# A streaming encoder layer on one core: a tile made 32 bytes longer, three stores on another queue, four row loads twenty ticks later

## The chip, the cores and the metric

The kernel runs on one core of one Trainium2 chip. The metric is the device time of one execution in microseconds (us), taken as the median of several runs. One core has five engines that the profile names: PE (matmuls), DVE and POOL (elementwise work), ACT (activations, casts and copies) and SP (which here only issues DMAs). Each engine carries out its own list of instructions in order, and a semaphore wait of one instruction holds back all that stand behind it on the same engine. An engine that issues a DMA has it in that list too. SBUF is the on-chip memory of 128 partitions; a tile's place is told as a byte offset within each partition. PSUM holds the results of matmuls in banks.

## The reference

One layer for 1152 rows of tokens: 1024 of one new stream and 8 times 16 of running streams, with a width of 1024. All is float32.

```
h = x @ w_in                                # one input projection: all branch columns and two merge gates
z, xbc, dt, q, k, v, f, g_path, mg_m, mg_a = split(h)
y_m = rmsnorm(ssd_scan(silu(conv(xbc)), softplus(dt)) * silu(z))    # Mamba-2 branch, width 2048
o   = softmax(q k^T / 8 + c_t - c_s) v                              # attention with forget gates, 16 heads
y_a = o * silu(g_path)                                              # width 1024
u   = sigmoid(mg_m + b) * (y_m @ w_br_m) + sigmoid(mg_a + b) * (y_a @ w_br_a)
out = layer_norm(alpha * x + u @ w_out)     # and k, v, log f, conv and SSD states as further outputs
```

## The kernel before, in words

**Products.** A float32 product is made of three matmuls. Each operand is split in a high part (a cast to the type fp32r) and a low part (the rest), and high x high, high x low and low x high are summed in one PSUM bank. So each weight tile needs a cast on ACT and a subtraction on DVE or POOL, and so does each tile of rows. `passes`, `dense`, `quarter` and `whole` make such products for 384 token columns at a time (there are three such column groups, c = 0, 1, 2); there the weights are the stationary operand and the rows the moving one.

**Stages, in PE's order.** (1) The value projection (L333 to L335): 432 matmuls of 128 x 512. Here X, the input, is stationary, and the moving operand is the value weight: `vh` and `vl`, the two parts of `wv`, 512 columns of one of them at a time. (2) Eight groups of the SSD scan, with the projections that they need (`d`, `z`, convolutions) and small float32 matmuls (`tp`, `dS`, `y`, `up`). (3) Eight head pairs of attention (`s`, `st`, `o`; for the running streams `ss`, `so`), among them the merge gates: `gate_dense(j)` multiplies X with one tile of gate weights, and for each column group ACT takes tanh from PSUM into a tile `gate` (L851), and SP stores it to DRAM as `gate_d` (L852). Gate 14 is the last of them in the attention loop, gate 15 follows after the loop's pools are closed. (4) The merge of the SSD branch: the first quarter of its sixteen row tiles (kt 8 to 11, `A0`, matmuls `dq`); then `unit()`, which multiplies the middle eight row tiles' quadrants in seven products where eight would be plain, in four parts p = 0 to 3 (matmuls u0d, u0m and so on to u3m); then the last quarter (kt 12 to 15, `A1`, `dq` again). (5) The attention branch's merge (`yb1`, L245 to L247 again). (6) The output projection (`out`, L1612 to L1614, 128 x 512 with u stationary and the weights `woh`, `wol` moving) and the layer norm.

**Order.** Nearly all of it runs in `tc.manual_schedule()`, which takes instructions in the order in which the code writes them; on each engine the program keeps that order. `flow` runs generators beside the products: every second k step of a product is one tick, and a generator that yields n gets on again n ticks later, so that its instructions are written between those of the product. A part p of `unit()` has 22 ticks, the unit 88.

**Pieces of weights in the unit.** `prepare()` makes one piece of the weight quadrants, 32 in all. The T pieces are first a difference of two quadrants (L1425; on POOL for p = 0, on DVE later); then ACT casts the high part (L1427) and POOL subtracts the low part (L1428). The raw weights `wu` of the next part are loaded by SP (L1410) once the pieces T4 and T3 of this part are made. What comes out of PSUM is added to `acc` by DVE (L1449).

**Rows of the last quarter.** `rows_c01` handles the row tiles kt = 12 to 15 during the unit. `send` (L1361, L1364) has SP load the rows `yr` and, for even kt, a row `rsb` of norm factors spread to all partitions; `scaled` (L1368, DVE) multiplies by them; `parted` (L1509 on ACT, L1510 on DVE) splits two of the three column groups in high and low part. They are read first by the `dq` matmuls behind the unit. For the first quarter `load_rows` does the like (L1276, L1281, L1288, L1304).

**Where tiles lie.** The pool `s1` gives out offsets one after another. `ones`, 32 floats a partition, stands ahead of `cw`, `cb`, `cst`, `ceo`, of the value weights and raw loads of stage 1, and of the SSD stage's tiles. All of these end with the SSD stage. The first of the value weights, vh for k = 0, begins at byte 105,344 of its partition, which is a multiple of 64; each of these tiles begins at a multiple of 64. X, the weight tiles `wh` and `wl`, and every tile of the later stages begin 32 bytes past one: `woh` and `wol` are among them. `pre` is a small tile of the attention's set-up at the start of the SSD stage: an exclusive running sum over eight blocks (L500 clears its first block), read once.

Of the kernel before, what the change touches and what calls it, by code (L numbers as in the profile page):

```python
# [11 lines left out]
F32 = mybir.dt.float32  # L12
# [7 lines left out]
P = 128  # L20
# [14 lines left out]
GATES_SSD = 4  # L35
GATES_FOX = 4
# [113 lines left out]
def trunk_step(ctx: ExitStack, tc: tile.TileContext, I, O):  # L150
    nc = tc.nc
    ve, ac, po, te, sy = nc.vector, nc.scalar, nc.gpsimd, nc.tensor, nc.sync
# [20 lines left out]
    def ch(c):  # L173
        return slice(c * CW, (c + 1) * CW)
# [11 lines left out]
    gate_d = dr.tile([16, P, T], F32, name="gate_d")  # L186
# [73 lines left out]
    def dense(rhs, evac):  # L260

        hi, lo = next_w()
        for c in range(NCH):
            d = bank(f"d{count[0]}_{c}")[:, :CW]
            passes(d, KT, lambda k: (hi[:, k * P:(k + 1) * P], lo[:, k * P:(k + 1) * P]),
                   lambda k: (rhs[c][0][:, k, :], rhs[c][1][:, k, :]), lambda: evac(c, d))
# [5 lines left out]
    s1 = ssd_stack.enter_context(tc.tile_pool(name="s1", bufs=1))  # L272
# [3 lines left out]
    ea = s1.tile([P, 8, 32], F32, name="ea")  # L276
    eas = s1.tile([P, 8, 32], F32, name="eas")
    xac = s1.tile([P, 32], F32, name="xac")
    ones = s1.tile([P, 32], F32, name="ones")
    cw = s1.tile([P, 32, 4], F32, name="cw")  # L280
    cb = s1.tile([P, 32], F32, name="cb")
    ncol = I["const"].shape[1]
# [9 lines left out]
    pp = pro_stack.enter_context(tc.tile_pool(name="pp", bufs=1, side="right"))  # L292
# [4 lines left out]
    sfx = pp.tile([P, SEQ + 1], F32, name="sfx")  # L297
    nsf = pp.tile([P, SEQ], F32, name="nsf")
    catm = pp.tile([P, 9, 48], F32, name="catm")
    ff = pp.tile([16, P], F32, name="ff")  # L300
    pre = pp.tile([P, 8, 16], F32, name="pre")
    acf = pp.tile([32, T], F32, name="acf")
    cpro = pp.tile([P, I["const2"].shape[1]], F32, name="cpro")
    fones = pp.tile([P, P], F32, name="fones")
# [539 lines left out]
        if g == 7:  # L844
            square_rows(g, square_sums(g, "t"))

    def gate_dense(j, pool, tag, bufs):

        def evac(c, d):
            t = pool.tile([P, CW], F32, tag=tag, name=f"gate{j}_{c}", bufs=bufs)  # L850
            ac.activation(t[:], d, AF.Tanh, bias=bcol[:, j:j + 1])  # L851
            sy.dma_start(gate_d[j][:, ch(c)], t[:])  # L852

        dense(X, evac)

# [6 lines left out]
    def q_and_gate(hp):  # L862

        fp = lazy["f0"] if hp % 2 == 0 else lazy["fp"]
        r = {}
        qh = r["qh"] = fp.tile([P, SEQ], F32R, tag="qh", name=f"qh{hp}", bufs=1)
        ql = r["ql"] = fp.tile([P, SEQ], F32R, tag="ql", name=f"ql{hp}", bufs=1)
        qbd = r["qbd"] = fp.tile([P, 8, 2, 16], F32, tag="qbd", name=f"qbd{hp}", bufs=1)
        po.memset(qbd[:], 0.0)

        def evac_q(c, d):
            a, b = halves(c)
            ac.copy(qh[:, b], d[:, a])
            ve.tensor_tensor(ql[:, b], d[:, a], qh[:, b].bitcast(F32), ALU.subtract)
            if c == 2:
                for e in range(2):
                    hr = slice(64 * e, 64 * e + 64)
                    ac.copy(qbd[hr, :, e, :], d[hr, 256:].rearrange("p (b w) -> p b w", w=16))

        dense(X, evac_q)  # L880
        gs = r["gs"] = (fp if hp % 2 == 0 else lazy["fq"]).tile([P, T], F32, tag="gs", name=f"gs{hp}", bufs=1)
        silu_dense(fp, None, None, None, whole=gs)
        return r

    def keys(hp, r):
        fp = lazy["fp"]
        kh = r["kh"] = fp.tile([P, SEQ], F32R, tag="kh", name=f"kh{hp}", bufs=1)
        kl = r["kl"] = fp.tile([P, SEQ], F32R, tag="kl", name=f"kl{hp}", bufs=1)
        knew = r["knew"] = fp.tile([P, P], F32, tag="knew", name=f"knew{hp}", bufs=2)

        def evac_k(c, d):
            a, b = halves(c)
            kf = fp.tile([P, CW], F32, tag="kv1", name=f"kf{hp}_{c}", bufs=3)
            ac.copy(kf[:], d)
            sy.dma_start(O["k"][hp][:, ch(c)], kf[:])
            if c == 2:
                po.tensor_copy(knew[:], kf[:, 256:])
            ac.copy(kh[:, b], d[:, a])
            ve.tensor_tensor(kl[:, b], d[:, a], kh[:, b].bitcast(F32), ALU.subtract)

        dense(X, evac_k)
        return r
# [313 lines left out]
    for j in range(GATES_SSD):  # L1216
        gate_dense(j, spa, "z", 9)
# [30 lines left out]
    with tc.manual_schedule():  # L1248
        r = keys(0, r)
        for hp in range(1, 8):  # L1250
            flow.start(pair(hp - 1, r))
            gate_dense(GATES_SSD + hp - 1, fp, "kv1", 3)
            r = keys(hp, q_and_gate(hp))
        flow.start(pair(7, r))
        for j in range(GATES_SSD + 7, GATES_SSD + 7 + GATES_FOX):
            gate_dense(j, fp, "kv1", 3)
        flow.drain()
    fp_stack.close()

# [98 lines left out]
    def send(kt, rb, pool=mp, tag="rsb"):  # L1358

        y = mp.tile([P, T], F32, tag="yr", name=f"yr1{kt}", bufs=4)  # L1360
        sy.dma_start(y[:], ym_d[kt])  # L1361
        if kt % 2 == 0:
            rb[0] = pool.tile([P, T], F32, tag=tag, name=f"rsb{kt}", bufs=1)
            sy.dma_start(rb[0][:], rs_d[kt // 2:kt // 2 + 1, :].to_broadcast([P, T]))  # L1364
        return y

    def scaled(kt, y, rb):
        ve.scalar_tensor_tensor(y[:], y[:], mcol[:, kt:kt + 1], rb[0][:], ALU.mult, ALU.mult)  # L1368
# [138 lines left out]
    def parted(i, c):  # L1507
        h, l = A1[c][0][:, i, :], A1[c][1][:, i, :]
        ac.copy(h, ys[i][:, ch(c)])  # L1509
        ve.tensor_tensor(l, ys[i][:, ch(c)], h.bitcast(F32), ALU.subtract)  # L1510

    def rows_c01():

        rb = [None]
        for kt in range(12, 16):
            ys.append(send(kt, rb))
            yield 6
            scaled(kt, ys[-1], rb)
            yield 4
            parted(kt - 12, 0)  # L1520
            parted(kt - 12, 1)
            yield 4

    def rows_c2():

# [4 lines left out]
    with tc.manual_schedule():  # L1530
        prepare()
        for i in range(4):
            put("S4", i, s4[i][:])
        flow.start(rows_c01())
        todo.pop(0)
        unit()
        flow.drain()
# [54 lines left out]
    for c in range(NCH):  # L1592
# [27 lines left out]
        for j in range(3):  # L1620
            b, w = 3 * c + j, width[j]
# [108 lines left out]
```

## Time and profile before

| | us |
|---|---|
| median of 3 runs | 2019.84 (2019.16 to 2020.88) |
| profiled execution, whole time | 2018.57 |
| its span, first instruction to last | 2016.7 |
| PE busy | 2005.7 (99%) |
| DVE, ACT, POOL busy | 1301.0, 913.5, 530.7 |
| value projection on PE | from about 10 to 115 |
| SSD stage | to about 963 |
| attention | to about 1600 |
| gate 15 and first quarter | to about 1668 |
| unit | to about 1762 |
| last quarter, attention merge | to about 1880 |
| output projection and layer norm | to 2016.7 |

In the lists of instructions the first number is the start in us from the start of the span, the second the time from start to end, for a group "x3" over all three. Brackets give the idle time ahead of an instruction and what ended it. Matmuls overlap: one that is shown with 0.34 us is followed by the next after 0.17, so that PE's pace is read from start to start. SPq and ACTq are the issuing of DMAs on SP and ACT; "DMA" in the chain of waits is the transfer.

### The profile page before, as it was taken

Reading aid. Unit: us, or ns where it says so; the run is one execution under the profiler, and the core shown is the slowest. Engines: PE = TensorE matmul, PEld = TensorE weight load, DVE = VectorE, ACT = ScalarE, POOL = GpSimd, SP = SyncE. Lnnn points to the kernel's source line nnn. Section 1 sums busy time; section 2 is a strip of 40 time slices with the busy share of each in tenths; the row PEclk is TensorE's granted clock in tenths of the full one; section 3 lists DMA queues with packets and bytes.
Section 4 is the critical chain, followed back from the end, with each engine's and each line's share of the span. In section 5 each row is a group of like instructions: output and inputs, shape, how many; then the busy total and the mean of one; then the engine's idle time right before and its main releaser. Section 6 shows DMA issues by size and latency. Waiting matters only on the chain.

```text
span 2016.7 us, 36178 instructions
## 1 busy us (share of the span) xinstructions
PE 2005.7 (99%) x14247; PEld 1859.7 (92%) x14247; DVE 1301.0 (65%) x2165; ACT 913.5 (45%) x1971; POOL 530.7 (26%) x708
## 2 busy tenths in 40 slices
PE   9999999999999999999999999999999999999998
PEld 7899999999999999999988988988888999999987
DVE  5145766766667676643577787787786687582355
ACT  5125555554655656543545545455545353221210
POOL 0012445354535454523011001000100005414400
PEclk9999999999999999999999999999999999999999
DMA  7422242424233323343566566566656573164322
GB/s 225 157 75 90 67 145 68 133 80 131 82 127 90 126 87 123 96 135 107 182 214 199 191 218 195 170 213 203 191 190 203 189 273 114 57 232 137 98 92 94
DMA packets 123627, 292.51 MB, mean 145 GB/s; under 512 B 18633, under 2 KB 74945, under 8 KB 113217
## 3 DMA queue, kind: packets, MB, share of 16 engines
q1 hardware_dynamic: 110912, 208.93, 32.4%
q10 hardware_dynamic: 12544, 81.27, 11.6%
q8 instruction: 112, 1.84, 0.4%
q14 instruction: 59, 0.48, 0.1%
HBM read 233.64 MB, written 56.51 MB: 144 GB/s over the span
## 4 chain that ended last, share of the span: by engine, by line
PE 92%; DVE 3%; ACT 1%; DMA 1%; issue 1%; POOL 1%; SPq 0%; ACTq 0%; DVEq 0%; POOLq 0%
PE d L245 19%; PE d L247 18%; PE d L246 18%; PE s L951 3%; PE o L1026 3%; PE dq L245 2%; PE y L736 2%; PE dq L247 2%; PE dq L246 2%; PE out L1614 2%; PE out L1613 2%; PE out L1612 2%; PE v L334 2%; PE v L335 2%; PE v L333 2%; PE so L1101 2%
## 5 line engine op out<-in xcount | busy, mean ns | idle before, releaser
L245 PE MATMUL d<-xh,wh 128*128 128x384 f32 x2112 | 735.6, 348 | 0.0
L247 PE MATMUL d<-xh,wl 128*128 128x384 f32 x2112 | 707.3, 335 | 0.0
L246 PE MATMUL d<-xl,wh 128*128 128x384 f32 x2112 | 706.7, 335 | 0.0
L245 PEld LDWEIGHTS d<-xh,wh 128*128 128x128 f32 x2112 | 396.7, 188 | 19.7 <-issue 8.1
L246 PEld LDWEIGHTS d<-xl,wh 128*128 128x128 f32 x2112 | 397.3, 188 | 0.8
L247 PEld LDWEIGHTS d<-xh,wl 128*128 128x128 f32 x2112 | 396.5, 188 | 0.0
L225 POOL TENSOR_TENSOR wl<-wr,wh 128x1024 fp32r<-128x1024 f32 x45 | 107.7, 2394 | 200.0 <-ACT wh L224 199.2
L956 ACT ACTIVATE st<-s,ckt 128x256 f32<-128x256 f32 (+1 forms) x320 | 115.1, 467 | 19.4 <-PE s L951 17.0
L224 ACT CAST wh<-wr 128x1024 fp32r<-128x1024 f32 x56 | 58.7, 1049 | 119.9 <-PE d L246 94.4
L1016 ACT ACTIVATE st<-st 128x1024 f32<-128x1024 f32 x80 | 83.2, 1062 | 38.9 <-DVE st L1011 36.2
L960 POOL TENSOR_TENSOR st<-st,mask_bf 128x256 f32<-128x256 f32 x64 | 49.3, 791 | 195.4 <-ACT st L956 195.3
L705 ACT ACTIVATE m<-ce,nacum 128x128 f32<-128x128 f32 x288 | 96.9, 391 | 5.7 <-PE y L736 5.7
L228 DVE SCALAR_TENSOR_TENSOR wl<-wr,wh 128x1024 fp32r<-128x1024 f32 x50 | 62.7, 1255 | 33.3 <-ACT wh L227 33.3
L1428 POOL TENSOR_TENSOR pc<-wu,pc 128x512 fp32r<-128x512 f32 x32 | 43.2, 1360 | 127.3 <-ACT pc L1427 127.3
L632 POOL TENSOR_TENSOR wx<-xdt,wdt 128x256 f32<-128x256 f32 x72 | 54.0, 751 | 84.7 <-DVE xdt L630 84.7
L1026 PE MATMUL o<-st,vt 128*64 128x256 f32 (+1 forms) x640 | 68.7, 362 | 0.2
L1026 PEld LDWEIGHTS o<-st,vt 128*64 128x64 f32 x640 | 43.1, 137 | 26.0 <-ACT st L1016 3.0
L245 PE MATMUL d<-yb1h,wh 128*128 128x384 f32 x192 | 64.1, 334 | 0.0
L246 PE MATMUL d<-yb1l,wh 128*128 128x384 f32 x192 | 64.1, 334 | 0.0
L247 PE MATMUL d<-yb1h,wl 128*128 128x384 f32 x192 | 64.1, 334 | 0.0
L227 ACT ACTIVATE wh<-wr 128x1024 fp32r<-128x1024 f32 x50 | 52.7, 1054 | 22.4 <-PE d L246 22.4
L851 ACT ACTIVATE gate<-d,bcol 128x384 f32<-128x384 f32 x48 | 27.8, 578 | 70.2 <-PE d L247 44.9
(773 smaller groups left out, 4175.5 us busy)
## 6 DMA issues: line engine op xcount, KB each, us to landing
wr<-in_wt SPq DMA_DIRECT2D x88, 512.0 KB
kc<-in_cache_k ACTq DMA_DIRECT2D x32, 1024.0 KB
vc<-in_cache_v ACTq DMA_DIRECT2D x32, 1024.0 KB
ce<-ac_d SPq DMA_DIRECT2D x96, 192.0 KB
gate_d<-gate SPq DMA_DIRECT2D x48, 192.0 KB
sb<-cs_d ACTq DMA_DIRECT2D x16, 576.0 KB
yr<-ym_d SPq DMA_DIRECT2D x16, 576.0 KB
g<-gate_d SPq DMA_DIRECT2D x48, 192.0 KB
```

The lines of the kernel that those rows point to most:

```text
L224: ac.copy(hi[:, :cols], raw[:, :cols])
L225: lazy.get("sub", po).tensor_tensor(lo[:, :cols], raw[:, :cols], hi[:, :cols].bitcast(F32), ALU.subtract)
L228: ve.scalar_tensor_tensor(lo[:, :cols], raw[:, :cols], scale, hi[:, :cols].bitcast(F32), ALU.mult, ALU.subtract)
L245: te.matmul(out, wh, xh, start=(k == 0), stop=False)
L246: te.matmul(out, wh, xl, start=False, stop=False)
L247: te.matmul(out, wl, xh, start=False, stop=(k == n - 1))
L632: po.tensor_tensor(wx[b][:], xdt[b][:], wdt[:, b, hs][:, :, None].to_broadcast([P, 4, 64]), ALU.mult)
L705: ac.activation(m[:, j, :], ce[:, j * P:(j + 1) * P], AF.Abs, bias=nacum[:, b, h:h + 1])
L951: te.matmul(ps2[:, e, 256 * x + q0:256 * x + 256], kk[hr, ks], qq[hr, qs], start=(at == 0), stop=(at == 2))
L956: ac.activation(S[j][:, e, kb, q0:], ps2[:, e, 256 * x + q0:256 * x + 256], AF.Identity, bias=ckt[:, kb, 2 * hp + e:2 * hp + e + 1])
L1016: ac.activation(w, w, AF.Exp, scale=-1.0)
L1026: te.matmul(o[64 * e:64 * e + 64, 256 * at + q0:256 * at + 256], vt[:, kb, 64 * e:64 * e + 64], S[j][:, e, kb, q0:256], start=(kb == 0), s ...
```

## The change

It has three parts.

1. `ones` takes 40 floats where it took 32, of which the first 32 are used. All tiles behind it in these pools lie 32 bytes further (928 tiles; eight more lie 512 bytes further): vh for k = 0 now begins at byte 105,376. To make room, `pre` has no tile of its own and lies in the first 512 bytes of `sfx`, which is free by then. So its clearing (L500) waits for POOL's negation of `sfx` (L475), and stands on DVE behind the sums that write `sfx` (L472), where it stood at DVE's start.
2. The three stores of gate 14 are issued by ACT, each behind its own tanh.
3. `rows_c01` begins with 20 ticks of nothing, and its steps take 12 ticks a row tile where they took 14: it ends after 68 of the unit's 88 ticks rather than 56.

```diff
-    ones = s1.tile([P, 32], F32, name="ones")
+    ones = s1.tile([P, 40], F32, name="ones")[:, 0:32]
...
-    pre = pp.tile([P, 8, 16], F32, name="pre")
+    pre = sfx[:, 0:P].rearrange("p (b c) -> p b c", c=16)
...
-    def gate_dense(j, pool, tag, bufs):
+    def gate_dense(j, pool, tag, bufs, queue=sy):
 
         def evac(c, d):
             t = pool.tile([P, CW], F32, tag=tag, name=f"gate{j}_{c}", bufs=bufs)
             ac.activation(t[:], d, AF.Tanh, bias=bcol[:, j:j + 1])
-            sy.dma_start(gate_d[j][:, ch(c)], t[:])
+            queue.dma_start(gate_d[j][:, ch(c)], t[:])
...
         for j in range(GATES_SSD + 7, GATES_SSD + 7 + GATES_FOX):
-            gate_dense(j, fp, "kv1", 3)
+            gate_dense(j, fp, "kv1", 3, ac if j == GATES_SSD + 6 + GATES_FOX else sy)
...
     def rows_c01():
 
         rb = [None]
+        yield 20
         for kt in range(12, 16):
             ys.append(send(kt, rb))
-            yield 6
+            yield 5
             scaled(kt, ys[-1], rb)
             yield 4
             parted(kt - 12, 0)
             parted(kt - 12, 1)
-            yield 4
+            yield 3
```

How the instructions stand on three engines. First SP at the end of attention, before. Names carry a running number behind the tile's own name; `gate_0` to `gate_2` behind `wr` are the column groups of gate 14, `yr` and `rsb` are the rows of the first quarter.

```order
L852 DMA gate_d<-gate_2_17414 128x384
L212 DMA wr_17421<-in_wbr 128x1024
L852 DMA gate_d<-gate_0_17470 128x384
L852 DMA gate_d<-gate_1_17500 128x384
L852 DMA gate_d<-gate_2_17593 128x384
L1276 DMA yr_17616<-ym_d 128x1152
L1281 DMA rsb_17618<-rs_d 128x1152
```

And ACT at the same place after the change, where `st` are attention weights, to which the exponential is applied (L1016):

```order
L1016 ACTIVATE st_1_17227<-st_1_17227 128x2x512
L851 ACTIVATE gate_0_17469<-d_0_17422,bcol 128x384
L852 DMA gate_d<-gate_0_17469 128x384
L1016 ACTIVATE st_1_17227<-st_1_17227 128x2x512 x2
L851 ACTIVATE gate_1_17499<-d_1_17473,bcol 128x384
L852 DMA gate_d<-gate_1_17499 128x384
L224 CAST wh_17627<-wr_17420 128x1024
L851 ACTIVATE gate_2_17592<-d_2_17567,bcol 128x384
L852 DMA gate_d<-gate_2_17592 128x384
```

The three stores have left SP, where `wr` is now followed by the first `yr`, and stand on ACT, one of them ahead of two exponentials.

DVE around the start of the unit's part p = 1, before. `wu` are weight quadrants (the last difference here makes the piece T4), and `yr` is kt = 13:

```order
L1425 TENSOR_TENSOR wu_0_18371<-wu_1_18408,wu_0_18371 128x512
L1368 SCALAR_TENSOR_TENSOR yr_18417<-yr_18417,mcol,rsb_18293 128x1152
L1449 TENSOR_TENSOR acc<-acc,u0m_18467 128x384 x2
L1425 TENSOR_TENSOR wu_0_18371<-wu_1_18408,wu_0_18371 128x512
L1510 TENSOR_TENSOR ya1l_18263<-yr_18417,ya1h_18262 128x384
L1510 TENSOR_TENSOR ya1l_18265<-yr_18417,ya1h_18264 128x384
L1449 TENSOR_TENSOR acc<-acc,u1m_18500 128x384 x4
L1425 TENSOR_TENSOR wu_0_18371<-wu_0_18371 128x512
```

And after, where `yr` is kt = 12:

```order
L1425 TENSOR_TENSOR wu_0_18365<-wu_1_18398,wu_0_18365 128x512
L1449 TENSOR_TENSOR acc<-acc,u0m_18455 128x384 x2
L1425 TENSOR_TENSOR wu_0_18365<-wu_1_18398,wu_0_18365 128x512
L1368 SCALAR_TENSOR_TENSOR yr_18462<-yr_18462,mcol,rsb_18464 128x1152
L1449 TENSOR_TENSOR acc<-acc,u1m_18491 128x384 x4
L1425 TENSOR_TENSOR wu_0_18365<-wu_0_18365 128x512
L1449 TENSOR_TENSOR acc<-acc,u1d_18478 128x384
L1510 TENSOR_TENSOR ya1l_18262<-yr_18462,ya1h_18261 128x384
L1510 TENSOR_TENSOR ya1l_18264<-yr_18462,ya1h_18263 128x384
```

Ahead of the difference for T4 there now stands the scaling of kt = 12, behind the difference for T2; the two subtractions of rows (L1510) stand behind it.

## The prediction

> **What bounds the kernel now.** I first read the page's head and its slices of the span (PEclk is the granted clock in tenths).
>
> ```profile
> span 2016.7 us, 36178 instructions
> PE 2005.7 (99%) x14247; PEld 1859.7 (92%) x14247; DVE 1301.0 (65%) x2165; ACT 913.5 (45%) x1971; POOL 530.7 (26%) x708
> PEclk9999999999999999999999999999999999999999
> ```
>
> PE works for 99% of the span at an even clock. So only two things can shorten it: fewer nanoseconds between matmuls that follow each other, or the few waits of PE. Against both I hold the three parts of the change. The list of PE's waits, by line, comes next; the columns are the total, the number and the longest.
>
> ```profile
> PE dq L245 <- ACT gate L851: 1.1, 1, 1.1
> PE u1m L1442 <- POOL pc L1428: 0.7, 1, 0.7
> PE u0m L1442 <- POOL pc L1428: 0.2, 1, 0.2
> ```
>
> These three lie behind 1600 us, where the second and third part of the change are. The first part has no wait to remove; for it I compared PE's pace in two stages with matmuls of the same size, 128x512, in the timeline: the value projection, whose moving operand lies at a multiple of 64 bytes, and the output projection, whose moving operand lies 32 bytes past one.
>
> ```profile
> L333 PE MATMUL v<-vh,xh 128*128 128x512 f32 x144 | 57.4, 399 | 0.0
> ```
> ```profile
> 20.09 0.40 PE L334 MATMUL v<-vl,xh 128*128 128x512 f32 x1
> ...
> 22.89 0.40 PE L334 MATMUL v<-vl,xh 128*128 128x512 f32 x1
> ...
> 1920.05 0.39 PE L1613 MATMUL out<-wol,uh 128*128 128x512 f32 x1
> ...
> 1922.77 0.39 PE L1613 MATMUL out<-wol,uh 128*128 128x512 f32 x1
> ```
>
> Each pair of rows is twelve matmuls apart. Value: (22.89 - 20.09) / 12 = 0.2333 us. Output: (1922.77 - 1920.05) / 12 = 0.2267 us. The same form takes 6.7 ns more in the value projection.
>
> **Part 1, the 32 bytes.** The stationary operand of both stages lies in the same place (u takes X's tiles), the type is the same, the clock too. What differs is the place of the moving operand, and the shift gives the value weights the output weights' place modulo 64. If the place makes the difference, the 3 x 144 matmuls gain 432 x 6.67 ns = 2.88 us. If it is something else (stage 1 has more DMA traffic), they gain 0. I take 2.88, since the pace was the same whichever twelve I took; 2.8 remain if the first 18 matmuls only reach the next value weight sooner. Below zero: matmuls of the SSD stage read shifted tiles too; that is the third rival.
>
> The Trainium skill speaks against this. "SBUF — State Buffer", section "Who interferes with whom", gives PE two read ports, one for the moving operand and one for loading weights, and lets PE wait for nobody; "TensorE: Matmul & The Clock Gate", Part 2, puts the gap of back-to-back matmuls at N/2.4 plus about 2.5 ns, 215.7 ns for 512 columns, whatever the place. By these both stages would show one number; the trace has 226.7 and 233.3, both above it. By the rule the first part is worth 0.
>
> The moved clearing of `pre` is not free in itself, since DVE now waits for POOL there:
>
> ```profile
> 133.89 2.78 POOL L475 TENSOR_SCALAR nsf<-sfx 128x1024 f32<-128x1024 f32 x1 [1.24 <-DVE sfx L472]
> 135.55 1.93 DVE L552 SCALAR_TENSOR_TENSOR acc0x<-raw0x,cw,acc0x 128x384 f32<-128x384 f32 x3 [1.75 <-ACT acc0x L541]
> ```
>
> POOL ends at 136.67, so the convolution steps queued behind on DVE start some 1.2 us later than 135.55. DVE had idled 1.75 us ahead of them and idles again between later groups; PE's banks there are emptied by ACT. I take 0; uncovered it would cost 1.2 us once.
>
> **Part 2, the stores of gate 14.** On SP the three stores stand ahead of the first rows of the next stage:
>
> ```profile
> 1593.01 12.49 SPq L852 DMA_DIRECT2D gate_d<-gate  x3
> ...
> 1606.02 1.32 SPq L1281 DMA_DIRECT2D rsb<-rs_d  x1
> ```
>
> SP is held until 1605.5 because the last store waits for the last tanh of gate 14. The rows themselves need the attention loop's memory, free when its last `so` is done. From the chain of waits in order of time (start, length):
>
> ```profile
> 1593.94 0.17 PE d L245
> ...
> 1597.30 2.10 PE so L1101 x72
> ...
> 1606.02 8.09 DMA rsb<-rs_d
> ```
>
> That is 1599.4. And this is what hangs on the transfer:
>
> ```profile
> 1614.26 2.93 DVE L1288 SCALAR_TENSOR_TENSOR yr<-yr,mcol,rsb 128x1152 f32<-128x1152 f32 x2 [5.41 <-DMA rsb<-rs_d]
> 1615.71 1.34 ACT L1304 CAST ya0h<-yr 128x384 fp32r<-128x384 f32 x3 [7.05 <-DVE yr L1288]
> 1616.95 0.57 ACT L851 ACTIVATE gate<-d,bcol 128x384 f32<-128x384 f32 x1
> 1616.14 0.34 PE L247 MATMUL d<-xh,wl 128*128 128x384 f32 x1
> 1617.58 0.44 PE L245 MATMUL dq<-ya0h,wh 128*128 128x384 f32 x1 [1.10 <-ACT gate L851]
> ```
>
> ACT stands with three casts waiting for DVE's scaling, and behind them in its list is the tanh that frees PE's bank. PE's usual step is 0.17 (the row of 1593.94); here it is 1617.58 - 1616.14 = 1.44, so 1.27 is lost, and 0.10 more as the first matmul after the pause takes 0.44 rather than 0.34: 1.37 us. With the stores gone `rsb` can be issued at about 1600.0, lands at 1608.1, is scaled to about 1610.3 (DVE first ends its own attention work near 1608.9) and cast by 1611.7. The tanh no longer stands behind anything late, and PE needs nothing of it before 1616.3: the whole 1.37 goes, with over 4 us to spare. What is late next: nothing that I see before the unit. Below, 0 remains if the rows still cannot start.
>
> The price is on ACT, where issuing takes
>
> ```profile
> 1577.97 0.33 ACTq L911 DMA_DIRECT2D vc<-in_cache_v  x1
> 1592.88 2.00 ACT L1016 ACTIVATE st<-st 128x1024 f32<-128x1024 f32 x2
> 1594.98 2.31 PE o L1026 x24
> ```
>
> 0.33 us each. The first store must let its own tanh end, at about 1593.0, and pushes the two exponentials queued behind it by about 0.57 us. PE's `o`, which begins at 1594.98, reads their halves at about 1595.5 and 1596.3, and they would end at 1594.5 and 1595.45: hidden by 0.8 us or more. The other two stores fall where ACT idles. I take 0; uncovered, 0.57 us.
>
> **Part 3, the rows of the last quarter.** In the unit PE waits twice for a piece of weights:
>
> ```profile
> 1688.65 0.34 PE L1441 MATMUL u0m<-S3l,pc 128*128 128x384 f32 x1
> 1689.19 0.45 PE L1442 MATMUL u0m<-S3h,pc 128*128 128x384 f32 x1 [0.20 <-POOL pc L1428]
> ...
> 1703.98 0.34 PE L1441 MATMUL u1m<-yb0l,pc 128*128 128x384 f32 x1
> 1705.06 0.44 PE L1442 MATMUL u1m<-yb0h,pc 128*128 128x384 f32 x1 [0.74 <-POOL pc L1428]
> ```
>
> Against the step of 0.17 these lose 0.37 and 0.91, and 0.11 and 0.10 in the first matmul after: 1.49 us. What makes the pieces late is the rows' work:
>
> ```profile
> 1676.96 2.14 DVE L1368 SCALAR_TENSOR_TENSOR yr<-yr,mcol,rsb 128x1152 f32<-128x1152 f32 x1
> 1677.97 2.29 POOL L1425 TENSOR_TENSOR wu<-wu,wu 128x512 f32<-128x512 f32 x1
> ...
> 1698.65 1.80 DVE L1510 TENSOR_TENSOR ya1l<-yr,ya1h 128x384 fp32r<-128x384 f32 x2 [1.16 <-ACT ya1h L1509]
> 1702.23 0.68 DVE L1425 TENSOR_TENSOR wu<-wu 128x512 f32<-128x512 f32 x1
> 1703.72 3.78 POOL L1428 TENSOR_TENSOR pc<-wu,pc 128x512 fp32r<-128x512 f32 x3 [4.15 <-ACT pc L1427]
> ```
>
> At p = 0 POOL's difference and DVE's scaling overlap and both are long; the twenty ticks move the rows out of p = 0 altogether. At p = 1 DVE waits 1.16 us for ACT, takes 1.80 for the rows, and only then gets to the sums and to T4's difference, which POOL's subtraction waits for. After the change only the scaling of kt = 12 stands ahead of T4. Its rows are issued behind the weight loads, near 1688.5, and the row loads of the unit take some 5.8 us from issue to use:
>
> ```profile
> 1705.88 0.43 SPq L1364 DMA_DIRECT2D rsb<-rs_d  x1
> 1711.66 2.18 DVE L1368 SCALAR_TENSOR_TENSOR yr<-yr,mcol,rsb 128x1152 f32<-128x1152 f32 x1 [3.61 <-DMA rsb<-rs_d]
> ```
>
> So the scaling can run from about 1695.2 (behind T2) to 1696.6 at 1.4 us, the four sums to 1698.5, T4's difference to 1699.2, and POOL's low part is there by about 1701.2. PE wants it at 1703.7 (0.17 behind 1703.98, less the 0.48 that the first wait no longer costs): 2.5 us to spare. Gain 1.49. Below: at p = 3 the rows of kt = 15 now come in front of T1's difference on DVE. Issued at about 1732.6, behind the weights, they land at 1738.4 at the latest by the 5.8, and the pieces T2 and T4 come 1.5 to 2 us ahead of their use. By the 8.09 us of the other stage's `rsb` they would be some 2.3 us later, and PE would lose up to 2.1.
>
> **The sum.** 2.88 + 1.37 + 1.49 = 5.7 us. The profiled execution took 2018.57, 1.27 less than the median of 2019.84, and would take 2012.8; the median would be **2014.1**.
>
> **The rivals.**
>
> 1. The place is not the cause of the 6.7 ns, and the shift does nothing. For it are these groups of PE, `y` of the SSD stage and `o` of attention, of which the former read tiles at multiples of 64 and the latter 32 bytes past one:
>
> ```profile
> L736 PE MATMUL y<-m,xdt 128*64 128x128 f32 x576 | 54.4, 277 | 0.0
> L740 PE MATMUL y<-ce,S 128*64 128x128 f32 x448 | 43.5, 273 | 0.0
> L1026 PE MATMUL o<-st,vt 128*64 128x128 f32 x128 | 12.4, 273 | 0.0
> ```
>
> They take 277, 273 and 273 ns, the same. Against it: this is another type and a quarter of the width, and no other stage has the value projection's pace. Time: 2019.84 - 1.37 - 1.49 = 2017.0. The rule from the Trainium skill's "SBUF — State Buffer", "Who interferes with whom", would come out here too.
> 2. A new wait at p = 3 takes the place of the removed ones, as worked out above: 5.7 - 2.1 = 3.6 gained, 2016.2. It decides once a row load in the unit takes over about 7.5 us. The rows seen there speak against it.
> 3. The other side. The place costs as I think but the other way round for float32 matmuls, which are split differently inside PE; those of the SSD stage that read shifted tiles pay the 6.67 ns. L736 and L740 alone are 1024 x 6.67 = 6.8 us, and the time 2014.1 + 6.8 = 2020.9. It turns the change to a loss from 860 matmuls on (5.7 / 0.00667); smaller groups would add to it. Against it: the attention row above, at 273 ns, is no slower than these two.
>
> That the shift doesn't reach the value weights is excluded by the tile offsets (105,344 and 105,376).
>
> **How the numbers follow.** My forecast 0.58, the first rival 0.26, the second 0.09, the third 0.07. A measurement of this kernel can tell about 0.2% from no change, 4.04 us, so faster begins below 2015.8. My forecast lies 1.7 us below that and clears it mostly (0.53 of its 0.58); of the first and second rival 0.02 and 0.02 do so too: faster 0.57. Same has the rest of these and half of the third: 0.39. Slower 0.04. The likeliest case alone spans 2013.0 to 2015.6 (0.7 us below by the rounding of the four starts, 36 x 0.02, and 0.4 by the spread of runs; 1.5 above by the clearing of `pre` uncovered and again the spread); with the first two rivals and the runs' own spread the range is 2012.8 to 2017.9.
>
> **What would show it.** Value matmuls: twelve in 2.72 us is right, 2.80 the first rival. SSD stage: `y` of L736 and L740 longer from start to start is the third rival. Gate 14: `rsb` issued near 1597 (1600.0 less the shift's gain) instead of 1606 and no bracket at the first `dq`; if SP still stands in front of it, the second part fails. Unit: no brackets at `u0m` and `u1m` is right; a bracket at u3m <- POOL pc is the second rival. The prediction is wrong if PE's wait only moves to another line, or if the pace of v is kept.

## The result

The changed kernel takes 2015.91 us (2014.78 to 2017.76 in 20 runs) against 2020.01 (2018.18 to 2023.05 in 20): 4.1 us less, a ratio of 0.9979 with a 95% interval of [0.9972, 0.9986]. That is faster, by 0.21%, where 0.28% had been forecast: the interval lies wholly below 1. The profiled executions differ by less, 2.66 us (2018.57 and 2015.91), for a reason that the stages show.

Head and engines of the page after:

```profile
span 2014.1 us, 36174 instructions
PE 2004.5 (100%) x14247; PEld 1861.9 (92%) x14247; DVE 1299.2 (65%) x2165; ACT 913.8 (45%) x1971; POOL 531.4 (26%) x708
```

The list of PE's waits after has nothing behind 1600 us any more; the first wait, at the start of the kernel, was 1.2 us before too:

```profile
PE warm L353 <- DVE sfx L465: 1.2, 1, 1.2
PE v L333 <- ACT vh L326: 0.7, 1, 0.7
PE tp L625 <- ACT bt L634: 0.2, 1, 0.2
PE v L334 <- DVE vl L327: 0.2, 1, 0.2
```

To see where the time went I laid PE's start times in both traces side by side, matmul by matmul, and summed the differences by stage (after less before): value projection -0.56 us, SSD stage +1.09, attention -0.07, all behind it -3.11; together -2.65. The value projection ends here with its last matmul, the SSD stage at 963 us of the kernel before.

**Behind attention.** The gate chain after, from the timelines of SP, ACT, DVE and PE:

```profile
1599.71 0.32 SPq L1276 DMA_DIRECT2D yr<-ym_d  x1
1600.08 0.42 SPq L1281 DMA_DIRECT2D rsb<-rs_d  x1
...
1592.89 0.56 ACT L851 ACTIVATE gate<-d,bcol 128x384 f32<-128x384 f32 x1
1593.48 0.33 ACTq L852 DMA_DIRECT2D gate_d<-gate  x1
1593.92 2.01 ACT L1016 ACTIVATE st<-st 128x1024 f32<-128x1024 f32 x2 [0.47 <-ACT gate L851]
...
1609.24 2.64 DVE L1288 SCALAR_TENSOR_TENSOR yr<-yr,mcol,rsb 128x1152 f32<-128x1152 f32 x2
...
1616.61 0.33 PE L247 MATMUL d<-xh,wl 128*128 128x384 f32 x1
1616.78 0.33 PE L245 MATMUL dq<-ya0h,wh 128*128 128x384 f32 x1
```

`rsb` is issued at 1600.08 rather than 1606.02, DVE scales at 1609.24 rather than 1614.26, and the first `dq` follows its neighbour after 0.17 us: the 1.37 us are gone. The two exponentials behind the first store end 3.04 us after the tanh ahead of it began (1592.89 to 1595.93), where it was 2.46 before (1592.42 to 1594.88): the store pushes them by 0.58 us, and no wait of PE's `o` is in the list. In the unit POOL's difference at p = 0 is short, and T4's difference on DVE comes early:

```profile
1676.39 1.29 POOL L1425 TENSOR_TENSOR wu<-wu,wu 128x512 f32<-128x512 f32 x1
...
1693.71 1.41 DVE L1368 SCALAR_TENSOR_TENSOR yr<-yr,mcol,rsb 128x1152 f32<-128x1152 f32 x1
1695.04 1.94 DVE L1449 TENSOR_TENSOR acc<-acc,u1m 128x384 f32<-128x384 f32 x4
1696.90 0.69 DVE L1425 TENSOR_TENSOR wu<-wu 128x512 f32<-128x512 f32 x1
```

T4's difference starts at 1696.90 where it started at 1702.23, and PE waits at neither `u0m` nor `u1m`.

**Value projection.** The timeline of PE after:

```profile
39.84 0.39 PE L335 MATMUL v<-vh,xl 128*128 128x512 f32 x1
...
48.08 0.39 PE L335 MATMUL v<-vh,xl 128*128 128x512 f32 x1
```

These rows are 36 apart: 8.24 / 36 = 0.2289 us. Before it was 0.2333, and 0.2267 was forecast. Over all 432 the shorter pace saves 1.82 us (start times summed against 226.7: 2.80 us over it before, 0.98 after). In the profiled execution 1.26 of this was lost again, 1.15 of it within the first twenty matmuls, where the second k step waited for ACT's casts, of which the first had waited 2.9 us for the load of `xr`:

```profile
9.48 0.40 PE L335 MATMUL v<-vh,xl 128*128 128x512 f32 x1
...
10.61 0.50 PE L333 MATMUL v<-vh,xh 128*128 128x512 f32 x1 [0.73 <-ACT vh L326]
```

That loss differs from execution to execution: with what the pace gains taken out, the value projection lost between -0.66 and +1.70 us against the profile before in the thirteen other profiles of this study (e5 and e12 below, which are one kernel, lost 1.70 and 1.02). It is why the two profiled executions differ by less than the medians.

**SSD stage.** A place at 203 us, the first projections behind three transposes (`tp`), before and after:

```profile
203.05 0.42 PE L245 MATMUL d<-xh,wh 128*128 128x384 f32 x1
203.31 0.34 PE L246 MATMUL d<-xl,wh 128*128 128x384 f32 x1
203.48 0.34 PE L247 MATMUL d<-xh,wl 128*128 128x384 f32 x1
203.66 0.33 PE L245 MATMUL d<-xh,wh 128*128 128x384 f32 x1
203.83 0.33 PE L246 MATMUL d<-xl,wh 128*128 128x384 f32 x1
204.00 0.33 PE L247 MATMUL d<-xh,wl 128*128 128x384 f32 x1
204.18 0.33 PE L245 MATMUL d<-xh,wh 128*128 128x384 f32 x1
```
```profile
202.50 0.42 PE L245 MATMUL d<-xh,wh 128*128 128x384 f32 x1
202.76 0.34 PE L246 MATMUL d<-xl,wh 128*128 128x384 f32 x1
202.94 0.35 PE L247 MATMUL d<-xh,wl 128*128 128x384 f32 x1
203.12 0.34 PE L245 MATMUL d<-xh,wh 128*128 128x384 f32 x1
203.30 0.34 PE L246 MATMUL d<-xl,wh 128*128 128x384 f32 x1
203.48 0.33 PE L247 MATMUL d<-xh,wl 128*128 128x384 f32 x1
203.65 0.33 PE L245 MATMUL d<-xh,wh 128*128 128x384 f32 x1
```

The first four steps behind the first one are 177, 185, 176 and 182 ns long after the change, and 174, 175, 173 and 173 before: 25 ns more, then the common 173. Steps of 180 to 186 ns between projections number 55 in the SSD stage before and 194 after. This place is one of the dearer ones: summed over the stage, in the changed kernel the projections behind the 72 groups of `tp` take 1.05 us more (15 ns a group) and those behind the 24 groups of `dS` 0.31, while those behind the 24 groups of `cb` take 0.26 less. The `y` matmuls, which the third rival named, keep their pace (43.5 and 43.6 ns from L736 to L736 on average). So the shift does cost something in the SSD stage, at the projections that follow a group of small matmuls and not at the small ones.

### The profile page after: what moved, and what is told of

It reads as the page before. It is cut to its first block, busy times and chain, and to the rows that moved or that the text cites. A ratio compares the mean times of both kernels' runs of the same rounds, so it can differ in the third digit from the quotient of the medians.

```text
span 2014.1 us, 36174 instructions
## 1 busy us (share of the span) xinstructions
PE 2004.5 (100%) x14247; PEld 1861.9 (92%) x14247; DVE 1299.2 (65%) x2165; ACT 913.8 (45%) x1971; POOL 531.4 (26%) x708
## 4 chain that ended last, share of the span: by engine, by line
PE 90%; DVE 5%; DMA 2%; ACT 1%; issue 1%; POOL 0%; SPq 0%; ACTq 0%; DVEq 0%; POOLq 0%
PE d L245 19%; PE d L247 18%; PE d L246 18%; PE s L951 3%; PE o L1026 2%; PE y L736 2%; PE dq L245 2%; PE dq L246 2%; PE dq L247 2%; PE out L1614 2%; PE out L1613 2%; PE out L1615 2%; PE v L334 2%; PE v L333 2%; PE v L335 2%; PE so L1101 1%
## 5 line engine op out<-in xcount | busy, mean ns | idle before, releaser
L1016 ACT ACTIVATE st<-st 128x1024 f32<-128x1024 f32 x80 | 83.2, 1062 | 40.9 <-DVE st L1011 38.0
```

Of the source, the lines that this page charges most:

```text
L1016: ac.activation(w, w, AF.Exp, scale=-1.0)
```

## The experiments

The theory from here on: places in SBUF set the pace of PE where nothing waits; the value matmuls gain, the SSD stage loses. Rivals: the pace of the value matmuls belongs to its stage, or comes out by chance; the SSD stage's loss is chance, or comes from the moved clearing. "Pace" is the mean from start to start in the middle of the stage, and stage times are against the profile before, as above. e7 to e11 ran once each, so they are read by stage and not by their whole time. In the six profiles whose SSD tiles lie as before (e5 to e9 and e12) the SSD stage differs by -0.13 to +0.16 us from the profile before, which is the scatter to hold its numbers against.

### The shift alone, and by other amounts

e1 is the kernel before with the 32 bytes and the view in `sfx` only. e2, e3 and e4 are the changed kernel with another length of `ones`:

```diff
-    ones = s1.tile([P, 40], F32, name="ones")[:, 0:32]
+    ones = s1.tile([P, 56], F32, name="ones")[:, 0:32]     # e2: 96 bytes; e3: 48 floats, 64 bytes; e4: 64 floats, 128 bytes
```

Expected of e1:

> The 32 bytes alone; the stores of gate 14 and the rows of the last quarter as before. Theory (the moving operand's place sets the pace): twelve value matmuls in 2.75 us as in the changed kernel (229 ns each, against 233 before), the waits at dq (1.1), u0m (0.2) and u1m (0.7) as before; 1.9 us less than before, 1.0 if the SSD stage's slower start of projections, which the changed kernel's trace shows, comes from the shift too. Rival (the pace comes from something else in the change): 233 ns, no gain.

Of e2:

> The changed kernel, but everything behind ones lies 96 bytes further than before instead of 32, so that the value weights begin 96 bytes past a multiple of 128, as the output weights do. Theory (place modulo 128): the value matmuls take the output projection's 226.7 ns, 1.0 us less in all than the changed kernel. Rival (the 2.3 ns that are left belong to the stage, to its transfers or casts): 229 ns, and the time of the changed kernel.

Of e3:

> The changed kernel with 64 bytes in place of 32. If the place modulo 64 decides, the value matmuls take 233.3 ns again and the gain of 1.9 us is lost; if the place modulo 128 decides in even steps, something between 229 and 226.7 ns.

Of e4:

> The changed kernel with 128 bytes in place of 32: a shift like the others, with the value weights at a multiple of 128 as before. Theory (place): 233.3 ns, 1.9 us slower than the changed kernel, and the SSD stage as before. Rival (not the place, but the tile that was given up, or the moved clearing): 229 ns.

Measured:

| | pace of v, ns | SSD stage, us | behind attention, us | ratio to before, 95% |
|---|---|---|---|---|
| before | 233.3 | 0 | 0 | 1 |
| e1, 32 bytes alone | 229.0 | +1.07 | -0.05 | 0.9992 [0.9984, 1.0001] |
| changed kernel, 32 bytes | 229.0 | +1.09 | -3.11 | 0.9979 [0.9972, 0.9986] |
| e3, 64 bytes | 233.3 | +0.62 | -3.11 | 0.9985 [0.9976, 0.9994] |
| e2, 96 bytes | 232.4, later 233.4 | +0.17 | -3.11 | 0.9983 [0.9974, 0.9992] |
| e4, 128 bytes | 234.3 | +0.11 | -3.11 | 0.9987 [0.9979, 0.9996] |

The same shift gives the same pace in two kernels, and other shifts give others, so it is the place and not the given-up tile or chance. But the theory of e2 falls: 96 bytes past a multiple of 128, just where the output weights lie, the value matmuls do not take 226.7 ns. Nor does the place modulo 64 decide alone (e1 and e2 are equal in it). The moving operand's own place is not enough.

### Equal places, and only the value weights by 32 bytes

What the output projection and the projections of 384 columns have in common is that moving and stationary operand begin at the same place modulo 512 bytes: X, u and all the weights lie at 96. The value weights lay at 384 before, 288 bytes past X. e5 leaves `ones` as it was and puts the value weights 224 bytes further, to 96 modulo 512; e6 puts them 32 bytes further:

```diff
-    wv = [(vp.tile([P, D], F32R, name=f"vh{k}"), vp.tile([P, D], F32R, name=f"vl{k}")) for k in range(KT)]
+    wv = [(vp.tile([P, D + 56 * (k == 0)], F32R, name=f"vh{k}"), vp.tile([P, D], F32R, name=f"vl{k}")) for k in range(KT)]
+    wv[0] = (wv[0][0][:, 56:D + 56], wv[0][1])             # e5; e6 with 8 for 56
```

> The changed kernel with ones at its old length, so that the SSD stage's tiles lie as before; only the value weights and the other tiles of the first stage lie 224 bytes further. Then moving and stationary operand of the value matmuls begin at the same place modulo 512 bytes (96), as in the output projection. Theory (the distance of moving and stationary operand modulo 512 decides, 0 gives 226.7 ns; 288, 320, 352, 384, 416 gave 233.3, 229, 233.3, 232.4 to 233.4 and 234.3): 226.7 ns, 2.9 us less than before in that stage; with the SSD stage as before and the 3.1 us behind attention, 6.0 us less than before. Rival (a stage's own rhythm, which no place brings to 226.7): 229 to 234 ns, 3 to 5 us less than before.

> The changed kernel with ones at its old length; only the value weights and the other tiles of the first stage lie 32 bytes further. Theory (the SSD stage's 0.9 us more come from its own tiles' place): 229 ns in the value matmuls, the SSD stage as before, 5.0 us less than before. Rival (they come from something else, such as the moved clearing): the SSD stage 0.9 us longer as in the changed kernel, 4.0 us less.

e5, rows of the timeline 36 matmuls apart:

```profile
40.02 0.39 PE L336 MATMUL v<-vh,xl 128*128 128x512 f32 x1
...
48.18 0.39 PE L336 MATMUL v<-vh,xl 128*128 128x512 f32 x1
```

8.16 / 36 = 0.2267 us: the output projection's pace, 2.63 us less over the stage than before. The SSD stage is as before (-0.01 us), the time behind attention 3.11 us shorter. In all 2013.83 us against 2020.44, a ratio of 0.9968 [0.9955, 0.9980]. e6 has 229.0 ns, the SSD stage at +0.15, and a ratio of 0.9975 [0.9965, 0.9986]. So the rhythm is not the stage's own, and the 1.09 us of the SSD stage come neither from the value weights nor from the moved clearing, which both kernels have.

### Which of the two operands

e10 moves X and all behind it by 224 bytes, so that the value weights lie where they lay in e5 but X doesn't; e9 is e5 with six output weights moved by 288 bytes:

```diff
+    xpad = ctx.enter_context(tc.tile_pool(name="xpad", bufs=1))
+    xpad.tile([P, 56], F32, name="xpad")
     xp = ctx.enter_context(tc.tile_pool(name="xp", bufs=1))
```
```diff
-            hi = op.tile([P, 1024], F32R, name=f"woh{k}")
+            hi = op.tile([P, 1024 + 72 * (k == 2)], F32R, name=f"woh{k}")[:, 72 * (k == 2):1024 + 72 * (k == 2)]
```

> The changed kernel with ones at its old length and X and all behind it 224 bytes further: the value weights lie at 96 modulo 512 as in the run with equal places, but X, the stationary operand, at 320. Theory (distance): 288 again, 233.3 ns in the value matmuls; in the output projection 226.7 where both moved, 233.3 for the last two weights, which did not. Rival (the moving operand's own place, 96, is the good one): 226.7 ns in the value matmuls, and the output's first six weights worse. Open for both: the projections of 384 columns, whose X now lies 224 bytes past the weights; if they were to pay 6.7 ns too, 6336 of them would take 42 us more.

> The kernel of the run before with equal places (value weights 224 bytes further), and the six output weights that have tiles of their own (k = 2 to 7) lie 288 bytes further, so that in 288 of the output projection's matmuls of 512 columns the moving operand begins 288 bytes past the place of the stationary one modulo 512, as the value weights did in the kernel before. Theory (the distance modulo 512 decides, in any stage): these take 233.3 ns, 1.9 us more in the output projection; those of the last two weights (wh, wl) keep 226.7. Rival (a matter of the first stage): all keep 226.7.

e10, twelve value matmuls:

```profile
39.96 0.39 PE L336 MATMUL v<-vl,xh 128*128 128x512 f32 x1
...
42.76 0.39 PE L336 MATMUL v<-vl,xh 128*128 128x512 f32 x1
```

2.80 / 12 = 0.2333: with the moving operand at the very place of e5 the pace is that of before, since the stationary one has moved. In its output projection the weights that moved along with u take 227.7 ns on average, where 226.7 had been expected, and the last two, which did not move, 233.4. e9, twelve of the output matmuls:

```profile
1920.00 0.39 PE L1615 MATMUL out<-wol,uh 128*128 128x512 f32 x1
...
1922.80 0.39 PE L1615 MATMUL out<-wol,uh 128*128 128x512 f32 x1
```

0.2333 again, in another stage, and 2.0 us more behind attention than in e5 (1.9 expected). The last two weights were to keep 226.7 and took 230.0; why is open, since their own place is unchanged. In both kernels the distance of the two operands is 288 bytes modulo 512, as in the kernel before, and the pace is 233.3 each time. At 384 columns the distance does next to nothing: X lay 224 bytes past the weights in e10, and the projections took 173.8 ns where they took 173.7. And the output's matmuls of 256 columns go the other way: at 288 bytes they take 117.5 ns in e9 and 117.8 in e10, at 0 bytes 120.0, so what a distance costs depends on the width. Distances between 0 and 224 bytes were not tried, and none but 0 and 288 at more than one pair of places. That it is a matter of modulo 512 is the simplest reading: moving the value weights 512 bytes changes nothing (e11 below), and modulo 64 or 128 is excluded (0 and 384 bytes are equal in both, with 226.7 and 232.4 ns), but no two of these distances differ by 256, so modulo 256 would fit as well.

### The SSD stage's tiles alone

e11 is the changed kernel with 120 for 56 in the lines of e5, so that the value weights lie 512 bytes further than before and only the SSD stage's tiles and what lies by them 32.

> The changed kernel, but the value weights and the other tiles of the first stage lie 512 bytes further than before instead of 32 (their distance modulo 512 is that of before), and only the rest behind ones, the SSD stage's tiles above all, 32. Theory: 233.3 ns in the value matmuls, and the SSD stage 0.9 us longer than before. Rival (the 0.9 us come from the first stage's tiles or from chance): the SSD stage as before within 0.3 us.

The value matmuls take 233.3 ns and the SSD stage 1.13 us more; steps of 180 to 186 ns number 206, where e5 has 50. With e5 and e6 this shows that the place of the SSD stage's own tiles, and the few that lie by them, makes the loss. The long steps are not all of it: in e10, where these tiles lie 224 bytes further, the stage takes 0.71 us more with 2 such steps. Which operand of which small matmul does it was not tried.

### The stores and the rows, each alone

e7 is the kernel before with `queue` for gate 14 (part 2 of the diff), e8 with the later rows (part 3).

> The kernel before with the three stores of gate 14 on ACT's queue alone. Theory: no wait at dq (1.1 before, 1.37 with the slow first matmul), the waits at u0m and u1m stay (0.2 and 0.7); the value matmuls at 233.3 ns again, since the place is that of before. Rival (the pace comes out differently from run to run): some other pace between 227 and 234 ns.

> The kernel before with the later rows of the last quarter alone. Theory: the wait at dq stays (1.1), the waits at u0m and u1m are gone and no other of 0.1 us or more comes, 1.7 us less behind attention; the value matmuls at 233.3 ns. Rival (the rows need the first rows of the merge to be early as well): a wait at u0m or u1m remains.

In e7 the wait at `dq` is gone and `u1m` waits 0.7 us as before; the 0.2 at `u0m`, expected to stay, is gone too (0.07 us is left in that step). Behind attention it takes 1.75 us less. In e8 both waits in the unit are gone, as expected, but so is most of the one at `dq`: 2.61 us less. The rows of e8, SP and DVE:

```profile
1609.03 0.43 SPq L1281 DMA_DIRECT2D rsb<-rs_d  x1
...
1614.51 1.42 DVE L1288 SCALAR_TENSOR_TENSOR yr<-yr,mcol,rsb 128x1152 f32<-128x1152 f32 x1 [3.88 <-DMA rsb<-rs_d]
```

The transfer took 5.5 us here, not 8.09, so that DVE scales only 0.25 us later than in the profile before, although `rsb` was issued 3.0 us later; PE's work ahead of `dq` ended 1.8 us later. In e1, which has the old stores too, it took 5.5 us as well, and there is no wait at the first `dq` either. It has larger ones in the unit, in its timeline of PE:

```profile
1690.40 0.45 PE L1442 MATMUL u0m<-S3h,pc 128*128 128x384 f32 x1 [0.74 <-POOL pc L1428]
...
1706.16 0.44 PE L1442 MATMUL u1m<-yb0h,pc 128*128 128x384 f32 x1 [0.73 <-POOL pc L1428]
```

Summed over start times, the steps that are longer than their form's pace behind attention come to 3.1 us in the profile before (1.37 at `dq`, 1.71 in the unit), 3.1 in e1 (0.5 and 2.6), 1.4 in e7 (all in the unit), 0.5 in e8 (all at `dq`) and nothing in the changed kernel. Between the profile before and e1, whose code is the same there, what PE doesn't wait for at `dq` it waits for in the unit; one pair doesn't show that this must be so. The two parts take away 3.1 us together in every profile that has both (e9 and e10 lose some of it again in the output projection), but how much each is worth alone came out differently with the transfer of the execution, and e7 and e8 are one execution each.

### The version that is faster than both

e12 is e5 once more, for its time.

> The kernel with equal places again, for its time against the kernel before: the 3.1 us behind attention, 2.7 us in the value matmuls and nothing lost in the SSD stage make 5.8 us less, a ratio of 0.9971; the changed kernel was measured at 0.9979. If its lower time was chance, it comes out at 0.9979 or above.

2013.70 us (2013.17 to 2014.88) against 2019.61: a ratio of 0.9971 [0.9958, 0.9983], as expected. It keeps parts 2 and 3 and the 226.7 ns, and leaves the SSD stage's tiles where they were. The interval overlaps that of the changed kernel, which was measured beside other runs of the kernel before; that it is faster than that one too rests on the stages (0.8 us in the value matmuls and 1.1 in the SSD stage) and on the times themselves: the slowest of the eleven runs of e5 and e12 took 2014.88 us, the fastest of the changed kernel's twenty 2014.78.

## Why the prediction was right, and where its sizes were not

It forecast 2014.1 us in a range of 2012.8 to 2017.9; 2015.91 lies in it, and the forecast gain of 5.7 us compares with 4.1. By its steps:

- **Part 1, 2.88 us: the place sets the pace, but the term is too large.** The step that failed is "the shift gives the value weights the output weights' place modulo 64". The place modulo 64 is not the condition. The distance from the stationary operand modulo 512 went from 288 to 320 bytes, where the pace is 229.0 ns, so that the term measured 1.82. Of the distances that were run only 0 gave 226.7, as in the output projection (e5; e9 and e10 take it away by moving one operand). That both stages share the stationary operand's place had been noted, and hid that the other operand's place counts only against it. That 32 bytes gained anything was luck: by the reasoning of the prediction 96 bytes would have done as well, and they gave 232.4 ns; of the four shifts that were run on all the tiles, 32 is the only one that gains more than 1 ns.
- **The first rival** (the shift does nothing) is excluded by e1 to e5, and with it what the Trainium skill's "SBUF — State Buffer", "Who interferes with whom", would make of it (two independent read ports of PE, so no part for places): the runs differ by up to 7.6 ns a matmul (226.7 to 234.3) with nothing changed but places.
- **The third rival** named the right stage and the wrong instructions and price: the SSD stage does pay, 1.1 us and not 6.8, in the projections behind small matmuls. The forecast left it out of the sum, and it should have been a term: 1.82 - 1.09 = 0.7 us is what the first part is worth by its stages. e1's ratio of 0.9992 [0.9984, 1.0001] agrees with that, but does not by itself show that the first part gains.
- **The moved clearing, 0**: right. In the changed kernel, where this place is reached 0.56 us sooner, POOL and DVE show:

```profile
133.33 2.78 POOL L475 TENSOR_SCALAR nsf<-sfx 128x1024 f32<-128x1024 f32 x1 [1.24 <-DVE sfx L472]
...
136.17 0.64 DVE L552 SCALAR_TENSOR_TENSOR acc0x<-raw0x,cw,acc0x 128x384 f32<-128x384 f32 x1 [2.92 <-issue]
```

  DVE's convolution step starts 2.84 us after POOL's negation where it was 1.66, so it is 1.2 us late, as worked out. No wait of PE appears, and the SSD stage of e5 and e6, which have the moved clearing, is as long as before within 0.15 us.
- **Part 2, 1.37 us**: right in the pair of profiles, by the chain foretold (`rsb` at 1600.08 where 1600.0 stood in the working, 1597 in the list of signs, which took off a gain that the starts and the SSD stage had used up). But the 8.09 us of the transfer were one execution's; 5.5 in e8. The price on ACT, 0.58 us where 0.57 had been worked out, was hidden.
- **Part 3, 1.49 us**: 1.71 with the smaller steps in the unit. DVE's order worked out as written down (scaling at 1693.71, T4's difference at 1696.90, forecast as 1695.2 and 1698.5 for the kernel without the other gains). **The second rival**, a wait at p = 3, did not come: `yr` of kt = 15 landed in time.

```profile
1729.90 0.43 SPq L1361 DMA_DIRECT2D yr<-ym_d  x1
...
1734.92 1.42 DVE L1368 SCALAR_TENSOR_TENSOR yr<-yr,mcol,rsb 128x1152 f32<-128x1152 f32 x1 [6.95 <-DMA yr<-ym_d]
```

That is 5.0 us from issue to use, where 5.8 had been assumed.

The sum by measured terms: 1.82 - 1.09 + 3.11 = 3.8, against the medians' 4.1. Of this parts 2 and 3 make 3.1, a little more than their forecast of 2.86; the first part makes 0.7 of 2.88. So the forecast of the time holds by the two parts whose mechanism was right and by the width of its range, in which 2017.0, with the first part at nothing, would have lain too.

## What to carry to other kernels

Where two stages with matmuls of one form have different paces at one clock, compare the places of both operands, not of one, and try making their distance zero; here that was worth 2.6 us in 110 (e5), while the changed kernel's 32 bytes, put on all the tiles behind as well, cost more than half of what they gave. Check each width by itself: matmuls of 256 columns went the other way here. A wait of PE whose length hangs on one transfer was worth, in these runs, what that transfer took in that execution; when several waits feed one another, size them together, from more than one profile.

## What the runs showed that was not expected

- The pace of 128x512 matmuls with nothing to wait for lay between 226.7 and 234.3 ns by the places of the operands: distance 0 modulo 512 (or 256, as said) gave 226.7 (227.7 in part of e10), 288 gave 233.3 or 233.4 in two stages and at two pairs of places, 320 gave 229.0, 352 gave 233.3, 384 gave 232.4 and later 233.4, 416 gave 234.3. Within a kernel it repeats in a fixed pattern of a few matmuls (in the changed kernel 229, 232, 226). What in PE makes it is not shown.
- Matmuls of 256 columns took 120.0 ns at distance 0 and 117.5 to 117.8 at 288. Matmuls of 384 columns hardly changed with the distance (173.7 and 173.8 ns), but took 15 ns more on average, 25 at the place shown, over the steps behind each group of `tp` whose tiles had moved by 32 bytes.
- Single profiles scatter by stage, also where the kernels do the same: by up to 2.4 us at the start of the value projection and up to 2.4 in attention (-0.30 to +2.11 against the profile before; e5 and e12, which are one kernel, +0.33 and +1.16). A change of 1 us can't be read from two spans, only from the stage in which it lies.
